# Gated linear attention's projections as seven block products in four passes over the tokens

## The chip, the cores and the metric

The kernel runs on one core of a Trainium2 chip. The metric is the device time of one execution in microseconds (us). The core has five engines, each with its own instruction queue: TensorE (PE; matmuls, with a sequencer that loads the held operand), VectorE (DVE), ScalarE (ACT), GpSimd (POOL) and SyncE (SP, which here issues almost all transfers). They meet through semaphores. Data lies in HBM and is moved to on-chip SBUF by 16 DMA engines; matmuls write to PSUM, 8 banks of 128 x 512 floats.

## What is computed

One layer, float32, on x of 2048 tokens by 1024. Attention first, then an FFN:

```python
h = rmsnorm(x, mix_norm_w)
q, k, v, r, glr = split(h @ w_in, [512, 1024, 2048, 3072])     # 4 heads, dk 128, dv 256, gate rank 16
log_a = log_sigmoid(glr @ w_gate2 + b_gate) / 16
g = cumsum of log_a within chunks of 64 tokens;  k_dec = k * exp(g_end - g)
for each chunk c:  state = state * exp(g_end[c]) + k_dec[c].T @ v[c];  o[c] = (q[c] / sqrt(128)) @ state
x = x + (rms_normalize(o) * norm_w * silu(r)) @ w_out
h = rmsnorm(x, ffn_norm_w);  u = causal_conv3(h @ w_up);  x = x + (silu(u[:2816]) * u[2816:]) @ w_down
out = rmsnorm(x, final_norm_w)
```

## The kernel before

Every float32 operand of a product is split into a high half in float32r and a low half, the rest (`split`, L206: a copy on ACT at L209, a subtraction on DVE at L210). A product then takes three matmuls per 128 of depth, high by low, low by high, high by high (`mm3`, L333; `mm3p`, L728).

Attention works on four blocks of 512 tokens. Per block x is normed and transposed (L354, L294), and its two halves stay in SBUF. Then for each head come r (`comp_r_tile`, tokens held, 256 columns moved; head 3 takes the gate's 16 columns along, 272), q (`comp_q`, weights held, 512 tokens moved) and k and v together (`comp_kv`, 384 columns). The weights are loaded and split anew for each block by `Weights` (L215), paced by a clock that `adv` moves on with each matmul (L315). The decay path (`phase_b2`, L384) turns gate values into factors and chunk sums. `scan_k` updates a head's state for the two chunks of a 128-token tile with two matmuls each, high and low half of k stacked in one operand; `scan_o` follows a delay of 4.5 us later (`later_do` with DLY), `scan_x` transposes the result for the output projection `comp_y` (L582), which runs in two halves of 512 columns. After the second half a tile is normed for the FFN, and `blocks` (L601) makes the seven operands of the FFN's products for a pair of tiles and stores them (`hd`, 14 stores of 256 KB).

The FFN already works in seven block products instead of eight: `phase_u` for up, conv and gate (two halves of 1024 tokens), then the down stage from `units` (L901) on. The tile scheduler adds the waits; each engine takes its instructions in the order in which the program emits them.

## Time and profile before

| | |
|---|---|
| median of 3 runs | 2247.65 us (2246.14 to 2248.06) |
| profiled execution, its own time | 2248.04 us |
| its span | 2246.3 us |
| granted TensorE clock, mean | 0.99 |
| attention, from the start to the first up product | 0 to 937.7 us |
| up stage | 937.7 to about 1816 us |
| down stage and final norm | about 1816 us to the end |
| DMA | 322.84 MB, mean 144 GB/s |

A group's row names a line, an engine, an operation, out<-in and a count, then busy us and the mean ns of one; behind the bar stands how long the engine had been idle before it, and who ended that. PE is TensorE's matmuls, PEld its weight loads. Matmuls overlap, so their mean is a latency; what one costs in a stream is the distance of two starts. L209 and L210 are the helper's lines, so their rows are told apart by the tiles.

### The profile page before, as it was taken

The page shows a single profiled execution, that of the slowest core. Times are in us where ns is not written, and L with a number is a line of the kernel's source. Part 1 is how long each engine was busy: PE and PEld are TensorE (multiplying, and loading weights), DVE is VectorE, ACT ScalarE, POOL GpSimd, SP SyncE. Part 2 cuts the span into 40 slices and gives each one's busy share as a digit, 9 for nine tenths or more (in the row PEclk, how much of TensorE's full clock was granted, in tenths as well). Part 3 has the DMA queues.
Part 4 walks back from the last instruction along what each step waited for, and adds up shares of the span by engine and source line. Part 5 has one row for each costly group of instructions (what it writes and reads, how often), then busy time and mean ns, then how long its engine had stood idle before and what let it go on. Part 6 is the DMA issues. An engine that isn't in the chain of part 4 may idle for free.

```text
span 2246.3 us, 31132 instructions
## 1 busy us (share of the span) xinstructions
PE 2172.5 (97%) x10909; PEld 1852.2 (82%) x10909; DVE 1519.6 (68%) x2337; ACT 1161.0 (52%) x2283; POOL 702.9 (31%) x639
## 2 busy tenths in 40 slices
...
GB/s 174 76 94 86 194 173 95 72 180 219 76 86 142 243 57 152 221 256 112 89 122 89 113 84 278 192 90 122 90 117 85 134 190 322 146 179 155 131 211 103
DMA packets 327886, 322.84 MB, mean 144 GB/s; under 512 B 15687, under 2 KB 262655, under 8 KB 324145
## 3 DMA queue, kind: packets, MB, share of 16 engines
...
q14 instruction: 73, 0.59, 0.1%
...
## 4 chain that ended last, share of the span: by engine, by line
PE 80%; DVE 7%; ACT 6%; issue 3%; DMA 3%; POOL 2%; SPq 0%; DVEq 0%; POOLq 0%; ACTq 0%
PE ua L733 7%; PE ua L734 7%; PE ua L735 7%; PE pd_p L735 6%; PE pd_p L734 6%; PE pd_p L733 6%; PE uc L733 4%; PE uc L734 3%; PE uc L735 3%; PE pkv L336 2%; PE pkv L338 2%; PE pkv L337 2%; PE pr L337 2%; PE pr L338 2%; PE pr L336 2%
## 5 line engine op out<-in xcount | busy, mean ns | idle before, releaser
L733 PE MATMUL ua<-h_p,uw_p 128*128 128x512 f32 x704 | 276.8, 393 | 1.2 <-DMA h_p<-hd_p 1.2
L735 PE MATMUL ua<-h_p,uw_p 128*128 128x512 f32 x704 | 276.3, 393 | 0.0
L734 PE MATMUL ua<-h_p,uw_p 128*128 128x512 f32 x704 | 276.2, 392 | 0.0
L806 DVE SCALAR_TENSOR_TENSOR t<-u,cw,t 128x1024 f32<-128x1024 f32 x176 | 244.2, 1418 | 40.4 <-ACT t L804 23.3
L735 PE MATMUL pd_p<-dw_p,da_p 128*128 128x512 f32 x616 | 239.6, 389 | 0.0
L734 PE MATMUL pd_p<-dw_p,da_p 128*128 128x512 f32 x616 | 239.6, 389 | 0.0
L733 PE MATMUL pd_p<-dw_p,da_p 128*128 128x512 f32 x616 | 239.6, 389 | 0.0
L210 DVE TENSOR_TENSOR uw_p<-us_p,uw_p 128x512 fp32r<-128x512 f32 x176 | 158.1, 900 | 118.4 <-ACT uw_p L209 118.4
L210 DVE TENSOR_TENSOR da_p<-da_p,da_p 128x512 fp32r<-128x512 f32 x154 | 127.7, 844 | 136.9 <-ACT da_p L209 134.8
L286 POOL TENSOR_TENSOR rstd_o<-var_o,neghalf 128x1 f32<-128x1 f32 x64 | 49.8, 778 | 535.2 <-DVE var_o L284 535.2
L209 ACT CAST uw_p<-us_p 128x512 fp32r<-128x512 f32 x176 | 108.5, 618 | 193.4 <-PE ua L734 75.5
L209 ACT CAST da_p<-da_p 128x512 fp32r<-128x512 f32 x154 | 94.1, 622 | 220.1 <-PE pd_p L734 171.1
L336 PE MATMUL pkv<-wl_q,hTh 128*128 128x384 f32 x512 | 172.6, 337 | 0.0
L338 PE MATMUL pkv<-wh_q,hTh 128*128 128x384 f32 x512 | 171.9, 336 | 0.0
L337 PE MATMUL pkv<-wh_q,hTl 128*128 128x384 f32 x512 | 171.5, 335 | 0.0
L733 PEld LDWEIGHTS ua<-h_p,uw_p 128*128 128x128 f32 x704 | 132.3, 188 | 31.8 <-issue 1.6
L735 PEld LDWEIGHTS ua<-h_p,uw_p 128*128 128x128 f32 x704 | 132.3, 188 | 30.1
L734 PEld LDWEIGHTS ua<-h_p,uw_p 128*128 128x128 f32 x704 | 132.3, 188 | 30.0
L733 PE MATMUL uc<-h_p,uw_p 128*128 128x512 f32 x352 | 142.4, 404 | 8.9 <-DVE u L886 7.7
L336 PE MATMUL pr<-wl_r,hTh 128*128 128x256 f32 (+1 forms) x512 | 150.1, 293 | 0.1
L337 PE MATMUL pr<-wh_r,hTl 128*128 128x256 f32 (+1 forms) x512 | 146.3, 286 | 0.4 <-DVE hTl L210 0.3
L210 DVE TENSOR_TENSOR uw_p<-ur,uw_p 128x512 fp32r<-128x512 f32 x132 | 129.3, 992 | 24.7 <-ACT uw_p L209 24.7
(208 smaller groups left out, 5661.2 us busy)
## 6 DMA issues: line engine op xcount, KB each, us to landing
...
da_p<-ad_p SPq DMA_DIRECT2D x154, 256.0 KB, 3.3
hd_p<-h_p SPq DMA_DIRECT2D x112, 256.0 KB, 3.6
...
ad_p<-as_p SPq DMA_DIRECT2D x88, 256.0 KB, 3.2
dr_p<-in_ffn_w_down_dram SPq DMA_DIRECT2D x77, 256.0 KB, 3.2
ad_p<-t SPq DMA_DIRECT2D x66, 256.0 KB, 4.6
raw_q<-in_gla_w_in_dram SPq DMA_DIRECT2D x128, 128.0 KB, 2.3
```

The costliest lines, as they stand in the source:

```text
L209: nc.scalar.copy(hi, src)
L210: nc.vector.tensor_sub(lo, src, f32(hi))
L286: nc.gpsimd.tensor_tensor(rstd, var, neghalf, op=ALU.pow)
L336: nc.tensor.matmul(ps_ap, ah, bl, start=(i == 0), stop=False)
L337: nc.tensor.matmul(ps_ap, al, bh, start=False, stop=False)
L338: nc.tensor.matmul(ps_ap, ah, bh, start=False, stop=(i == n - 1))
L733: nc.tensor.matmul(ps_ap, ah, bl, start=(first and i == 0), stop=False, **kw)
L734: nc.tensor.matmul(ps_ap, al, bh, start=False, stop=False, **kw)
L735: nc.tensor.matmul(ps_ap, ah, bh, start=False, stop=(last and i == len(pairs) - 1), **kw)
L806: nc.vector.scalar_tensor_tensor(t, u[:, k:k + TS], cw[:, k, c:c + 1], t, op0=ALU.mult, op1=ALU.add)
```

## The change

Attention runs as four passes over all 2048 tokens: R (r and the gate), A (k, q, v of heads 0 and 1), B (heads 2 and 3), Y (output). A pass has 1024 columns and a depth of 1024, both cut in two; with a pair of token tiles that is a 2 x 2 x 2 block product, taken as seven products (p1 to p7) of sums and differences of blocks, 12 matmuls each. `prep_w` makes a pass's seven weight operands (sums on POOL, splits on ACT and DVE), which stay in SBUF for the pass's eight units; in the last unit of a pass each is replaced by the next pass's, as its product is done. `prep_row` makes the token side: in R from the normed x, stored to HBM as well (`h1d`), in A and B by loading these, in Y from the attention rows. r, the decay factors and the attention rows go through HBM (`rd`, `ed`, `od`). The gate gets matmuls of its own (`gate_mm`), the chunk sums as well (`sums`). The scan takes two heads of a tile at once: three matmuls per head and chunk for the state, and q is transposed from rows (`scan_tile`). The norm weight is multiplied into silu(r) on POOL instead of into the output weights. The FFN keeps its order; its operand ring has 6 pairs (18 single buffers before), its activations lie in the buffers that held the passes' weights and are loaded in the last Y unit.

```diff
-    HEADS = [3, 0, 1, 2]
-    WB = 18
-    SB = 13
...
+    NTT = S // P
+    NP = NTT // 2
+    WB = 6
+    RB = 4
+    SB = 8
+    YB = 7
+    LEAD = 4
+    DLY = 4.5
+    TX0, TX = (16.4, 18.6), (10.8, 13.5)
...
-    class Weights:
...
-    def comp_r_tile(b, h, hT, tt, rs):
-        pr = mm_ps(f"pr_{b}_{h}_{tt}")
...
-    def comp_q(b, h, hT):
-        pq = mm_ps(f"pq_{b}_{h}")
-        mm3(pq, KT, ((w_q(b, h, kt, 0, DK), hs(hT, kt, slice(0, T))) for kt in range(KT)))
...
-    def scan_k(b, h, tt, n, kk, vv, vl, dec, rs, oT):
-        S_ = []
-        for c in range(2):
-            pk = aux_ps(f"pk_{n}_{c}")
-            nc.tensor.matmul(pk[:, :DV], kk[:, c, :], vl[:, c, :], start=True, stop=False)
-            nc.tensor.matmul(pk[:, :DV], kk[:, c, :], vv[:, c, :], start=False, stop=True)
...
+    def w_block(ps_, i, j):
+        ks = slice(HK * j, HK * (j + 1))
+        if ps_ == "R":
+            return [(0, wv[:, ks, OR + 512 * i:OR + 512 * (i + 1)])]
+        if ps_ == "Y":
+            return [(0, wov[:, ks, 512 * i:512 * (i + 1)])]
+        g = "AB".index(ps_)
+        if i == 1:
+            return [(0, wv[:, ks, OV + 512 * g:OV + 512 * (g + 1)])]
+        return [(0, wv[:, ks, OK_ + 256 * g:OK_ + 256 * (g + 1)]), (256, wv[:, ks, OQ + 256 * g:OQ + 256 * (g + 1)])]
...
+    WSRC = {"p1": ((0, 0),), "p5": ((1, 0), (1, 1)), "p6": ((0, 0),), "p2": ((0, 1),), "p3": (), "p7": ((0, 0), (1, 0)), "p4": ((1, 1),)}
+    WHALF = [(o, k, ij) for o in PORD for k in range(2) for ij in WSRC[o]]
...
+    def load_w(ps_, n):
+        while wload.get(ps_, 0) < min(n, len(WHALF)):
+            m = wload.get(ps_, 0)
+            o, k, ij = WHALF[m]
+            r = wgot[ps_, o, k, ij] = raw_tile([P, 2, 512], f"wr_{ps_}_{m}")
+            for c, src in w_block(ps_, *ij):
+                nc.sync.dma_start(r[:, :, c:c + src.shape[-1]], src[:, 2 * k:2 * k + 2, :])
+            wload[ps_] = m + 1
...
+    def stage_w(ps_, o, ijs):
+        t = uh.tile([P, KT, 512], F32, tag=o, name=f"ws_{ps_}_{o}", bufs=1)
+        for n, ij in enumerate(ijs):
+            for c, src in w_block(ps_, *ij):
+                nc.sync.dma_start(t[:, n * HK:(n + 1) * HK, c:c + src.shape[-1]], src)
+            staged[ij] = t[:, n * HK:(n + 1) * HK, :]
...
+    def prep_w(ps_, o):
+        t = uh.tile([P, KT, 512], F32R, tag=o, name=f"w_{ps_}_{o}", bufs=1)
+        hi, lo = t[:, :HK, :], t[:, HK:, :]
+        for k in range(2):
+            v = (slice(None), slice(2 * k, 2 * k + 2))
+            r = [wgot.pop((ps_, o, k, ij)) if (ps_, o, k, ij) in wgot else staged[ij][v] for ij in WSRC[o]]
+            src = xsum[v]
+            if o == "p5":
+                nc.gpsimd.tensor_add(src, *r)
+            elif o == "p6":
+                nc.gpsimd.tensor_sub(src, src, r[0])
+            elif o == "p7":
+                nc.gpsimd.tensor_sub(r[1], *r)
+                src = r[1]
+            elif o != "p3":
+                src = r[0]
+            split(hi[v], lo[v], src)
+            if o == "p2":
+                nc.gpsimd.tensor_sub(xsum[v], r[0], xsum[v])
+        W[ps_, o] = (hi, lo)
...
+    def split_row(ps_, j, o, src):
+        t = w_pair(f"h_{ps_}{j}_{o}")
+        split(t[:, 0, :], t[:, 1, :], src)
+        if ps_ == "R":
+            nc.sync.dma_start(h1d[j, o], f32(t))
+        rows[ps_, j, o] = t[:, 0, :], t[:, 1, :]
...
+    def norm_x(t):
+        xt = xin[t]
+        junk = gp.tile([P, 1024], BF16, tag="cp", name=f"junk_{t}", bufs=4)
+        rstd = rstd_of(xt, D, f"a{t}", junk, "a")
+        nc.vector.scalar_tensor_tensor(xt, xt, rstd, rp["nw"], op0=ALU.mult, op1=ALU.mult)
...
+        b11, b21 = hsrc.pop(("t", t - 1))
+        b12, b22 = hsrc.pop(("t", t))
+        t1 = diff(j, "p5", b12, b11)
+        t2 = diff(j, "p6", b22, t1)
+        diff(j, "p7", b22, b12)
+        hsrc[j, "p3"] = b22
+        hsrc["p4", j] = (b21, t2)
...
+    def prep_row(ps_, j, o):
+        if ps_ == "R":
+            need(f"h{j}")
+            if o == "p4":
+                diff(j, o, *hsrc.pop(("p4", j)))
+            split_row(ps_, j, o, hsrc.pop((j, o)))
+        elif ps_ in "AB":
+            t = w_pair(f"h_{ps_}{j}_{o}")
+            nc.sync.dma_start(f32(t), h1d[j, o])
+            rows[ps_, j, o] = t[:, 0, :], t[:, 1, :]
...
+                t = oraw[j, o] = cp_tile(f"ot_{j}_{o}")
+                a, c = {"p5": (b12, b11), "p6": (b22, oraw.get((j, "p5"))), "p7": (b22, b12), "p4": (b21, oraw.get((j, "p6")))}[o]
+                nc.gpsimd.tensor_sub(t, a, c)
+            else:
+                t = {"p1": b11, "p2": b21, "p3": b22}[o]
+            split_row(ps_, j, o, t)
...
+    def gate_mm(j, o, hh, hl):
+        if o not in ("p1", "p5", "p2", "p3"):
+            return
+        GR = 2 * RANK
...
+        k0 = HK if o in ("p2", "p3") else 0
+        for c in {"p1": (0, 1), "p5": (1,), "p2": (0,), "p3": (1,)}[o]:
+            out = pg[:GR, c * P:(c + 1) * P]
+            kw = {} if o == "p1" and c == 0 else {"skip_group_check": True}
+            for k in range(HK):
+                ks = slice(k * P, (k + 1) * P)
+                nc.tensor.matmul(out, wg[:, 1, k0 + k, :], hl[:, ks], start=(o == "p1" and c == 0 and k == 0), stop=False, **kw)
+                nc.tensor.matmul(out, wg[:, 0, k0 + k, :], hh[:, ks], start=False, stop=(k == HK - 1), **kw)
...
+            for h in range(H):
+                for i in range(2):
+                    nc.tensor.matmul(pe[:, 2 * h:2 * h + 2], L[tt][1 - i][:, h * DK:(h + 1) * DK], rp["chunk"], start=(i == 0), stop=(i == 1))
...
+    def scan_loads(g, t):
+        e = sp["a"].tile([P, 2 * DK], F32, tag="E", name=f"E_{g}_{t}", bufs=2)
...
+        r = sp["a"].tile([P, 512], F32, tag="r", name=f"r_{g}_{t}", bufs=2)
+        nc.sync.dma_start(r, rd[t][g])
+        nc.scalar.activation(r, r, AF.Silu)
+        nc.gpsimd.tensor_mul(r, r, sp["gnw"])
+        er[t] = e, r
...
+        def first():
+            e, box["r"] = er.pop(t)
+            kd = sp["a"].tile([P, 2 * DK], F32, tag="kd", name=f"kd_{n}", bufs=1)
+            nc.vector.tensor_mul(kd, kq[:, :2 * DK], e)
+            for c in range(2):
+                own = slice(c * CH, (c + 1) * CH)
+                split(kz[0][own, c, :], kz[1][own, c, :], kd[own, :])
+            pq = aux_ps(f"pq_{n}")
+            for h in range(2):
+                nc.tensor.transpose(pq[:, h * P:(h + 1) * P], kq[:, (2 + h) * DK:(3 + h) * DK], ident)
...
+        def scan_k():
+            state = sp["state"]
+            for c in range(2):
+                pk = aux_ps(f"pk_{n}_{c}")
+                for h in range(2):
+                    kh, kl = (kz[i][:, c, h * DK:(h + 1) * DK] for i in range(2))
+                    vh, vl = (v[i][:, h * DV:(h + 1) * DV] for i in range(2))
+                    o = pk[:, h * DV:(h + 1) * DV]
+                    nc.tensor.matmul(o, kh, vl, start=True, stop=False)
+                    nc.tensor.matmul(o, kl, vh, start=False, stop=False)
+                    nc.tensor.matmul(o, kh, vh, start=False, stop=True)
+                    adv(0.36)
...
+                for h in range(2):
+                    nc.vector.scalar_tensor_tensor(state[:, h, :], state[:, h, :], dec[:, 2 * g + h, ci:ci + 1], pk[:, h * DV:(h + 1) * DV], op0=ALU.mult, op1=ALU.add)
+                sh = sp["b"].tile([P, 2, DV], F32R, tag=f"sh{c}", name=f"sh_{n}_{c}", bufs=1)
+                sl = sp["b"].tile([P, 2, DV], F32R, tag=f"sl{c}", name=f"sl_{n}_{c}", bufs=1)
+                split(sh, sl, state)
+                S_.append((sh, sl))
+            later_do(DLY, scan_o)
...
+        def scan_o():
+            po = aux_ps(f"po_{n}")
+            for h in range(2):
+                pairs = [((q[0][:, h, c * CH:c * CH + P], q[1][:, h, c * CH:c * CH + P]), (S_[c][0][:, h, :], S_[c][1][:, h, :])) for c in range(2)]
+                mm3p(po[:, h * DV:(h + 1) * DV], pairs)
...
+    def unit(ps_, j):
...
+        first = ps_ == "R" and j == 0
+        if ps_ == "R":
+            if first:
+                wload[ps_] = len(WHALF) - 2
+                load_w(ps_, len(WHALF))
+            elif j + 2 < NP:
+                for t in (e + 4, d + 4):
+                    xin[t] = load_x(t, "x")
+            if j + 1 < NP:
+                for i, t in enumerate((e + 2, d + 2)):
+                    norm_x(t)
+                    later_do((TX0 if first else TX)[i], lambda t=t: blocks_x(t))
...
+        if ps_ == "Y":
+            xe, xd = xin.pop(e), xin.pop(d)
...
+        if j + 1 == NP and nxt:
+            load_w(nxt, RB)
+        for i, o in enumerate(PORD):
+            if first:
+                for m in range(WEARLY[i], WEARLY[i + 1]):
+                    prep_w(ps_, PORD[m])
+                    prep_rows(m + 1)
+            prep_rows(limit(ps_, j, i))
...
+            hh, hl = rows.pop((ps_, j, o))
+            wh, wl = W[ps_, o]
+            pairs = [((hh[:, k * P:(k + 1) * P], hl[:, k * P:(k + 1) * P]), (wh[:, k, :], wl[:, k, :])) for k in range(HK)]
+            if o in ("p1", "p5", "p2"):
+                a = bank[o] = mm_ps(f"m{o}_{ps_}_{j}")
...
+            else:
+                a = bank["p5" if o == "p3" else "p1"]
+                mm3p(a, pairs, first=False, more=True)
+            if ps_ == "R":
+                gate_mm(j, o, hh, hl)
+            if j + 1 == NP:
+                if nxt:
+                    load_w(nxt, WEND[i - 1] + RB if i else 0)
+                    prep_w(nxt, o)
...
+                else:
+                    load_op(0, o)
+                    if i == 3:
...
+            if ps_ == "Y":
+                for xt, cs in {"p1": ((xe, c1),), "p5": ((xd, c2),), "p6": ((xd, c1),), "p2": ((xe, c1),),
+                               "p7": ((xd, c2),), "p3": ((xd, c1),), "p4": ((xe, c2),)}[o]:
+                    add(xt[:, cs], xt[:, cs], a)
+                if o == "p7":
+                    x1_done(d, xd)
+                if o == "p4":
+                    x1_done(e, xe)
+                continue
...
+            if o in ("p1", "p5", "p6"):
+                keep[o] = cp_tile(f"c{o}_{ps_}_{j}")
+                nc.scalar.copy(keep[o], a)
+            elif o == "p2":
...
+                elif o == "p4":
+                    ve = scan_v(g, e, a)
+                    scan_loads(g, d)
+                    if j > 0 or g > 0:
+                        need(*(f"scan{g if j else 0}_{(e - 1 - k) % NTT}" for k in range(2)))
+                    if j == 0:
+                        scan_b(g)
+                    later_do(0.2, lambda: scan_tile(g, e, o11, ve, lambda: scan_tile(g, d, o12, keep["vd"], lambda: None)))
...
+    rp["h"] = rp["hctx"].enter_context(tc.tile_pool(name="rh", bufs=1, side="right"))
+    rp["nw"] = rp["h"].tile([P, D], F32, name="nw_mix")
+    nc.sync.dma_start(rp["nw"], mix_norm_w.partition_broadcast(P))
+    xin[1] = load_x(1, "x")
...
+    stage_w("R", "p4", ((0, 0), (1, 0)))
+    stage_w("R", "p7", ((1, 1), (0, 1)))
+    gate_weights()
+    xin[2], xin[3] = load_x(2, "x"), load_x(3, "x")
+    for t in range(2):
+        norm_x(t)
...
+    nc.gpsimd.memset(halo, 0.0)
+    later_do(12.0, vectors)
+    for ps_ in PS:
```

917 lines of the change are left out of this document (413 added, 504 removed).

## The prediction

> **What bounds the kernel now.** The page was read first (its busy table and its chain of waits), then the busy time by stretches of the span, then the groups by line, then single instructions in order of time.
>
> ```profile
> span 2246.3 us, 31132 instructions
> ...
> PE 2172.5 (97%) x10909; PEld 1852.2 (82%) x10909; DVE 1519.6 (68%) x2337; ACT 1161.0 (52%) x2283; POOL 702.9 (31%) x639
> ...
> PE 80%; DVE 7%; ACT 6%; issue 3%; DMA 3%; POOL 2%; SPq 0%; DVEq 0%; POOLq 0%; ACTq 0%
> ```
>
> TensorE is the bound: 97% busy and 80% of the chain. Attention ends where the first FFN product starts, at 937.7 us (the tile ua's row: ns, then first and last start):
>
> ```profile
> L733 PE MATMUL ua<-h_p,uw_p x704: 387/392/632, 937.7 to 1812.7; 128*128 128x512 f32 x176
> ```
>
> The stretches (columns: time, then busy us and instructions of PE, weight loads, DVE, ACT and POOL, granted clock, DMA share, GB/s):
>
> ```profile
> 0.00:20.00 20.00, 9.30 (x54) 8.78 (x55) 10.70 (x21) 11.12 (x23) 8.96 (x34) 1.00 0.88 267
> 20.00:40.00 20.00, 19.65 (x123) 17.11 (x122) 11.95 (x32) 15.36 (x34) 0.93 (x1) 1.00 0.70 208
> ...
> 260.00:270.00 10.00, 7.07 (x25) 4.12 (x23) 9.23 (x12) 8.18 (x17) 3.09 (x3) 0.77 0.94 267
> 270.00:280.00 10.00, 9.08 (x40) 7.24 (x41) 5.56 (x11) 5.08 (x11) 2.62 (x2) 0.71 0.98 292
> 280.00:290.00 10.00, 8.85 (x51) 8.45 (x50) 8.17 (x15) 6.12 (x15) 3.75 (x3) 1.00 1.12 333
> ...
> 0.00:938.00 938.00, 891.13 (x5351) 807.75 (x5352) 613.86 (x1334) 578.68 (x1381) 123.13 (x156) 0.99 0.44 137
> ...
> 937.00:1040.00 103.00, 87.54 (x360) 69.92 (x359) 80.41 (x78) 47.20 (x76) 55.02 (x47) 0.92 0.65 205
> 1040.00:1800.00 760.00, 756.67 (x3276) 613.25 (x3275) 569.40 (x586) 374.36 (x551) 407.98 (x348) 1.00 0.39 124
> ```
>
> A busy figure counts overlapping latencies, so what a matmul costs is read from start to start. The FFN's up stage, which already works in seven block products, gives 760/3276 = 0.232 us per 512-wide matmul. Attention's own, from matmuls in a row (start, duration, line, operands), and their numbers from the groups:
>
> ```profile
> 52.71 0.41 PE L434 MATMUL pdec<-ident,dc 8*128 8x8 f32 x4 [0.22 <-ACT dc L428]
> ...
> 130.01 0.33 PE L336 MATMUL pkv<-wl_q,hTh 128*128 128x384 f32 x1
> ...
> 131.91 0.33 PE L338 MATMUL pkv<-wh_q,hTh 128*128 128x384 f32 x1
> ...
> 899.56 0.28 PE L337 MATMUL po<-sh,qlo 128*128 128x256 f32 x1
> ...
> 900.15 0.40 PE L336 MATMUL py<-wl_o,oTh 128*128 128x512 f32 x1
> ...
> 904.79 0.40 PE L338 MATMUL py<-wh_o,oTh 128*128 128x512 f32 x1
> 905.03 0.38 PE L577 MATMUL px<-ident,og 128*128 128x128 f32 x2
> 905.17 0.48 PE L336 MATMUL py<-wl_o,oTh 128*128 128x512 f32 x1
> ```
>
> ```profile
> L336 PE MATMUL pkv<-wl_q,hTh 128*128 128x384 f32 x512 | 172.6, 337 | 0.0
> ...
> L336 PE MATMUL pr<-wl_r,hTh 128*128 128x256 f32 (+1 forms) x512 | 150.1, 293 | 0.1
> ...
> L336 PE MATMUL py<-wl_o,oTh 128*128 128x512 f32 x256 | 103.1, 405 | 0.2
> ...
> L337 PE MATMUL pq<-hTh,wl_q 128*128 128x512 f32 x128 | 53.7, 419 | 10.3 <-DVE wl_q L210 10.3
> ...
> L336 PE MATMUL po<-sl,qhi 128*128 128x256 f32 x128 | 38.8, 303 | 9.6 <-DVE sl L210 7.6 <-DVE var_a L284 1.5 <-DVE var_o L284 0.4
> ...
> L554 PE MATMUL pk<-vlz,kk 128*128 128x256 f32 x128 | 35.0, 293 | 5.0 <-DVE vlz L547 3.8 <-DVE state L558 0.9
> ...
> L577 PE MATMUL px<-ident,og 128*128 128x128 f32 x128 | 25.3, 276 | 1.2 <-DVE og L571 1.2
> ...
> L607 PE MATMUL pt_d<-ident,h 128*128 128x128 f32 x128 | 18.8, 289 | 13.5 <-DVE h L598 10.6 <-DVE var_d L284 3.0
> ...
> L423 PE MATMUL pge<-ll,inchunk 128*8 128x512 f32 x16 | 7.0, 435 | 0.0
> ...
> L434 PE MATMUL pdec<-ident,dc 8*128 8x8 f32 x16 | 1.6, 207 | 0.2 <-ACT dc L428 0.2
> ```
>
> So: 384 wide, 11 steps in 1.90 us, 0.173; 256 wide, 5 steps in 0.59, 0.118; 512 wide, 20 steps in 4.64, 0.232; two transposes 0.14; the smallest, (0.41 - 0.207)/3 = 0.068. At these prices attention holds 836 us of TensorE work: 1536 k-v matmuls 265, 1536 gate-branch ones (taken as 256 wide) 181, 768 output ones 178, 384 q ones 89, 384 + 256 of the scan 76, 128 scan transposes 9 and 256 token transposes 18, 80 of the decay path 19, 16 small 1. It takes 938, so **102 us are lost** to waits and to a lowered clock: the start, and above all the block ends, where the output projection, the FFN's operands and their stores meet (260 to 280 us: clock 0.77 and 0.71, DMA share 0.94 and 0.98).
>
> **The change part by part.** *Projections.* Seven products of 12 matmuls for two token tiles by 1024 columns, 32 such units: 2688 matmuls of 512 columns at 0.232 = 624 us, against 265 + 181 + 178 + 89 = 713. **-89.**
>
> *Scan of two heads.* Its output matmuls stay 384; the state products go from 256 to 384, since the high and low halves of k are no longer stacked in one operand: 128 x 0.118 = +15. q now leaves the product with tokens on the partitions and is transposed: 64, in pairs of 0.14, +4.5.
>
> *Gate.* The gate's 16 columns leave the product and become 320 matmuls, 128 wide with 32 columns held. No row shows this form. Below it stands the smallest matmul, 0.068 (22 us), above it the 256-wide one, 0.118 (38), or at the very worst the 512-wide one, 0.232 (74). I take 0.068, as the 256-wide one is twice the columns. The chunk sums become 128 matmuls of two columns (0.068, +9) for 32 of 512 (-7) and 16 transposes (-1). Together +23. TensorE's work thus falls by 89 - 15 - 4.5 - 23 = **-46 us**, to 790.
>
> By the Trainium skill, "TensorE: Matmul & The Clock Gate", section Back-to-back issue gap, pairs of weight load and matmul sustain about 81 ns at 128 columns; the small transposes here show 68 ns; by the page's figure the gate would be 4 us dearer, an estimate, and the sum the same within its range.
>
> What is lost to waits comes anew, from these prices (the second fence is from the transfers: KB of one, us to landing):
>
> ```profile
> L210 DVE TENSOR_TENSOR uw_p<-ur,uw_p 128x512 fp32r<-128x512 f32 x132 | 129.3, 992 | 24.7 <-ACT uw_p L209 24.7
> ...
> L209 ACT CAST uw_p<-us_p 128x512 fp32r<-128x512 f32 x176 | 108.5, 618 | 193.4 <-PE ua L734 75.5 <-PE ub L734 40.0 <-POOL us_p L762 37.3
> ...
> L210 DVE TENSOR_TENSOR wl_q<-raw_q,wh_q 128x512 fp32r<-128x512 f32 x128 | 89.1, 710 | 7.5 <-ACT wh_q L209 5.5 <-PE pr L338 0.2
> ...
> L762 POOL TENSOR_TENSOR us_p<-ur 128x512 f32<-128x512 f32 x44 | 75.6, 1719 | 25.8 <-DMA ur<-in_ffn_w_up_dram 16.7 <-DVE uw_p L210 8.7
> ...
> L558 DVE SCALAR_TENSOR_TENSOR state<-state,dec,pk 128x256 f32<-128x256 f32 x128 | 60.7, 474 | 2.8
> ...
> L762 POOL TENSOR_TENSOR us_p<-ur,ur 128x512 f32<-128x512 f32 x44 | 60.3, 1374 | 19.5 <-DVE uw_p L210 19.5
> ...
> L210 DVE TENSOR_TENSOR h_p<-ht_p,h_p 128x512 fp32r<-128x512 f32 x32 | 33.8, 1055 | 3.3 <-ACT h_p L209 1.6 <-DMA hd_p<-h_p 0.6
> ...
> L598 DVE SCALAR_TENSOR_TENSOR h<-x,rstd_d,nw_ffn 128x1024 f32<-128x1024 f32 x16 | 26.7, 1666 | 10.1 <-POOL rstd_d L286 10.1
> ...
> L593 DVE TENSOR_TENSOR x<-x,py 128x512 f32<-128x512 f32 x32 | 21.9, 683 | 20.6 <-PE py L338 20.3
> ```
>
> ```profile
> hd_p<-h_p SPq DMA_DIRECT2D x112, 256.0 KB, 3.6
> ```
>
> *The start.* ACT and POOL get the norms of tiles 2 and 3 ahead of the first weights (`norm_x` stands before the loop in `unit`), and SP issues those two loads behind 4.2 MB of weights: 7.0 MB in all, at 267 GB/s from 2 us on, 28 us. Only then come the splits and POOL's chain of weight sums (p5, p6, the sum behind p2, p7): 8 halves of 2 x 1.37 to 2 x 1.72, some 3.1 us each, 25 us. First product near 31, p7 near 57, the unit's end near 61, for 26 us of TensorE work: **35 lost.** It is bounded below by 20 (the loads alone), above by 50 (POOL at 1.72, and the products, which wait in turn, at a lowered clock). The old start lost its share too; it is in the 102.
>
> *Pass changes (R to A, A to B, B to Y).* In the last unit of a pass the next pass's weights are made: 16 loads of 512 KB through four buffers, 14 splits of 1024 columns, POOL's 25 us. SP's loads wait for a buffer that POOL frees; queued behind them are the operand rows of the next unit, which TensorE needs. DVE has 14 x 1.3 = 18 us more there, on top of a unit's own work in a window of 26. Spread over two units it nearly fits; the rest falls on scans that wait for DVE. From 0 (all hidden) to 18 each; I take 20 for the three.
>
> *The Y pass.* A unit is 84 x 0.232 + 16 transposes, 20.6 us of TensorE. DVE has 7 row splits at 0.95 (between 0.71 and 0.99, nearer the row with POOL at work), 7 adds at 0.68, two norms at 1.67, 7 operand splits at 1.06: 22 us. DMA has 6.8 MB (7 x 512 KB of FFN operands, 1 MB each of attention rows, x and its sum's store; one store of 256 KB lands in 3.6 us): at 290 GB/s 23.5. Both above TensorE, so a unit takes 25: 8 x 4.4 = **35 lost**; from 0 to 64 (28.7 us, 6.8 MB at 238 GB/s, the mean of the first two stretches).
>
> *The scan's wait.* A scan tile now updates two heads: per chunk two state updates of 0.474, a split of 0.618 and 0.71, twice 2.28 = 4.6 us in a row on DVE and ACT, where one head took half; the delay before the output matmuls is still 4.5 us of TensorE work, and behind a waiting output matmul stands the next unit's product. Before, the output matmuls waited 9.6 us for 64 heads' tiles (row of po). For 32 double tiles I bound it by 0 and 32 (1 us each) and take 0.3 each, 10; with 2 for other gaps in R, A and B, **12 lost**.
>
> Lost: 35 + 20 + 35 + 12 = 102, as before by chance; the block ends go, and a dearer start and pass changes come. The early FFN (937 to 1040: 360 matmuls, 84 us' worth, in 103) I leave alone: its operands now load in the last Y unit, whose 15 MB crowd the same queue. The FFN's shorter ring, six pairs for nine, has five jobs of lead, 14 us, as its cover; without it DVE's stalls would show, 750 us of matmuls at 1% being 8. **Sum: -46**, from the profiled execution's 2248.0 us (2246.3 is its span; the median of the runs is 2247.65): **2202 us.**
>
> **The rivals.** *A, the losses fall.* If Y is bound by TensorE and the pass changes hide, 35 + 12 + 5 are lost instead of 102: 2152. For it: DVE is at 65% and POOL at 13% over 0 to 938 us, so there is room on average. Against it: the Y pass, where three engines stand at their limits in one window.
>
> *B, slower: transfers bind attention.* Operand rows are stored and read twice, gates, r and attention rows go out and back, weights come four times. By the shapes that is 50 MB in R, 40 each in A and B, 55 in Y and 30 of weights: 215 MB, against 938 x 137 = 128 MB now, all on SP's queue. It decides where the queue carries less than 215 MB / 942 us = 228 GB/s. At 220 attention takes 977 us: 2287. For it: 208 GB/s at 20 to 40 us. Against it: 333 at 280 to 290, and 267 to 292 where stores of the same kind press.
>
> *C, no change: the weights' preparation paces the pass changes.* POOL and DVE then sit at their upper prices at the start and at all three changes: 50 + 54 + 35 + 12 = 151 lost, 2251. For it: POOL's 1.72 and DVE's 0.99 are what the up stage pays when both work. Against it: the next pass's first products need only the first weights, so most of the chain has a second unit to finish in.
>
> That the change does not shorten TensorE's list of projections at all can be left out: the numbers of matmuls are fixed by the loops.
>
> **How the numbers follow.** Forecast 0.57, A 0.21, B 0.16, C 0.06 (the likeliest decides the time). About 0.2%, 4.5 us, is what a measurement of this kernel tells from no change. Faster: forecast and A, 0.78; same: C, 0.06; slower: B, 0.16. The likeliest case by itself spans 2165 to 2240, with the bounds of start, changes and Y partly offsetting. The range reaches past A below, and above past C and a gate at its worst (52 more, 2254) towards B: 2145 to 2262.
>
> **What would show it.** Right: attention's end near 890 us; 2688 projection matmuls near 0.23 us start to start; the first one near 31 us, with ACT waiting for the x loads; POOL as the releaser of p5 to p7 in the first 60 us; in the Y pass DVE over 85% busy and a DMA share over 0.9. Wrong: gate matmuls over 0.12 us; a DMA share near 1 in the A and B passes with TensorE waiting for operand rows (B); a Y unit near 21 us (A); an up stage longer than 880 us.

## The result, and the profile after

The change makes the kernel slower: 2361.43 us (2359.31 to 2364.44) against 2247.86 us, a ratio of 1.0508 with an interval of 1.049 to 1.0526. The forecast was 2202 us, faster. The page of the kernel after (span; busy time; shares of the chain of waits):

```profile
span 2357.6 us, 28614 instructions
...
PE 2142.0 (91%) x9948; PEld 1764.0 (75%) x9948; DVE 1571.2 (67%) x1967; ACT 1052.0 (45%) x1837; POOL 926.2 (39%) x730
...
PE 47%; DVE 6%; DMA 3%; issue 3%; POOL 2%; ACT 2%; SPq 0%; DVEq 0%; POOLq 0%; ACTq 0%
```

TensorE has less to do (2142 us busy for 2172, 961 matmuls fewer), yet it is 91% busy instead of 97%. The shares of the chain can't be set against the 80% of before: here they add up to 63%, since the chain could be followed back only as far as about 865 us, into the Y pass. The stretches by stage, from the starts of the first products (columns as in the prediction: time, then busy us and instructions of PE, weight loads, DVE, ACT and POOL, granted clock, DMA share, GB/s). The rows are the start (first unit of R), the rest of R, A, B, Y, the first 92 us of the up stage, its rest, and the down stage:

```profile
0.00:73.60 73.60, 36.53 (x160) 28.10 (x161) 59.79 (x55) 28.91 (x40) 42.68 (x36) 0.79 0.51 181
73.60:300.40 226.80, 198.48 (x1089) 162.29 (x1089) 124.84 (x156) 118.38 (x207) 63.14 (x45) 0.92 0.62 222
300.40:533.70 233.30, 215.99 (x1121) 183.31 (x1120) 129.76 (x250) 114.05 (x245) 50.74 (x44) 0.96 0.64 210
533.70:782.30 248.60, 225.76 (x1180) 190.65 (x1179) 151.89 (x295) 112.94 (x261) 61.71 (x45) 0.96 0.61 203
782.30:1004.00 221.70, 185.67 (x832) 150.03 (x831) 159.84 (x209) 98.25 (x178) 101.75 (x77) 0.93 0.73 236
1004.00:1096.00 92.00, 61.12 (x257) 48.93 (x256) 50.38 (x55) 35.71 (x58) 34.70 (x33) 0.83 0.71 236
1096.00:1927.40 831.40, 796.58 (x3458) 651.75 (x3457) 635.79 (x624) 398.17 (x587) 448.11 (x365) 0.99 0.39 124
1927.40:2357.60 430.20, 421.90 (x1861) 348.96 (x1860) 258.88 (x328) 145.62 (x263) 123.35 (x89) 0.99 0.51 175
```

And the up and down stages before:

```profile
937.70:1030.00 92.30, 81.19 (x344) 64.85 (x342) 70.66 (x70) 43.74 (x72) 48.72 (x42) 0.94 0.68 217
1030.00:1816.20 786.20, 778.52 (x3357) 630.86 (x3358) 590.60 (x611) 386.20 (x568) 413.57 (x354) 1.00 0.39 125
1816.20:2246.30 430.10, 422.00 (x1861) 348.95 (x1859) 244.83 (x325) 152.42 (x264) 117.72 (x89) 0.99 0.51 178
```

Attention ends at 1004.0 instead of 937.7 us: +66. The up stage takes 923.4 us instead of 878.5: +45. The down stage is the same. That is the whole 111 us by which the spans differ. What TensorE waits for (releaser: us in total, times, longest):

```profile
PE mp_Y L170 <- DVE x L786: 30.5, 7, 5.8
PE px L609 <- DVE og L602: 30.4, 19, 6.6
PE uc L170 <- DVE u L969: 30.2, 20, 2.8
PE ua L170 <- ACT uw_p L177: 19.1, 1, 19.1
PE pz L448 <- ACT gstk L432: 14.7, 4, 7.3
...
PE pg L424 <- DVE wg L392: 10.8, 1, 10.8
```

There is no single large wait but some in each stage: Y, the scan, the up stage in its course and at its head, the gate in R, the start. And a wait can cost more than its length. Two instances, in R and in Y (start, duration, line, operands; in brackets the idle time and its releaser), where the product p4 waits for the reading of p7 (in Y the scheduler has put half a dozen matmuls of the next unit between the two):

```profile
131.05 0.39 PE L170 MATMUL mp_R<-w_R_p,h_R_p 128*128 128x512 f32 x1
133.82 0.80 PE L170 MATMUL mp_R<-w_R_p,h_R_p 128*128 128x512 f32 x1 [2.38 <-DVE o_R L741]
134.42 0.63 PE L171 MATMUL mp_R<-w_R_p,h_R_p 128*128 128x512 f32 x1
...
136.55 0.63 PE L170 MATMUL mp_R<-w_R_p,h_R_p 128*128 128x512 f32 x1
...
883.95 0.39 PE L170 MATMUL mp_Y<-w_Y_p,h_Y_p 128*128 128x512 f32 x1
...
889.16 0.39 PE L172 MATMUL mp_Y<-w_Y_p,h_Y_p 128*128 128x512 f32 x1
894.74 0.74 PE L170 MATMUL mp_Y<-w_Y_p,h_Y_p 128*128 128x512 f32 x1 [5.19 <-DVE x L786]
```

Before the wait in Y, 23 steps take 5.21 us, 0.227 each. After the wait in R, five steps take 2.13 us from 134.42 on, 0.43 each: the granted clock is 0.50 from 133.66 to 137.07 us, so the pause of 2.4 costs 1.5 us more.

At the prediction's way of pricing (start to start: 0.228 for 512 columns, 0.119 for 256, 0.06 to 0.11 for the small ones) attention holds about 782 us of matmuls, against the forecast's 790. It takes 1004, so **222 us are lost where 102 were forecast**: start 48, rest of R 50, A 30, B 38, Y 56 (length of the stage less its matmuls' price).

### The profile page after: what moved, and what is told of

It is laid out like the page before. It is cut to its first block, busy times and chain, and to the rows that moved or that the text cites. A ratio compares the mean times of both kernels' runs of the same rounds, so it can differ in the third digit from the quotient of the medians.

```text
span 2357.6 us, 28614 instructions
## 1 busy us (share of the span) xinstructions
PE 2142.0 (91%) x9948; PEld 1764.0 (75%) x9948; DVE 1571.2 (67%) x1967; ACT 1052.0 (45%) x1837; POOL 926.2 (39%) x730
## 2 busy tenths in 40 slices
DMA packets 320640, 415.39 MB, mean 176 GB/s; under 512 B 19166, under 2 KB 212878, under 8 KB 316912
## 3 DMA queue, kind: packets, MB, share of 16 engines
q8 instruction: 78, 1.28, 0.2%
## 4 chain that ended last, share of the span: by engine, by line
PE 47%; DVE 6%; DMA 3%; issue 3%; POOL 2%; ACT 2%; SPq 0%; DVEq 0%; POOLq 0%; ACTq 0%
PE pd_p L171 6%; PE pd_p L170 6%; PE pd_p L172 6%; PE ua L172 5%; PE ua L171 5%; PE ua L170 5%; PE uc L170 3%; DVE t L896 3%; PE uc L171 3%; PE uc L172 3%; PE ub L172 2%; PE ub L170 2%; PE ub L171 2%; DVE uw_p L178 1%; DMA ur<-in_ffn_w_up_dram 1%
## 5 line engine op out<-in xcount | busy, mean ns | idle before, releaser
L170 PE MATMUL ua<-h_p,uw_p 128*128 128x512 f32 x704 | 276.8, 393 | 35.5 <-ACT uw_p L177 19.1
L896 DVE SCALAR_TENSOR_TENSOR t<-u,cw,t 128x1024 f32<-128x1024 f32 x176 | 261.3, 1513 | 21.7 <-POOL halo L892 9.4
L170 PE MATMUL pd_p<-dw_p,da 128*128 128x512 f32 x616 | 239.6, 389 | 0.0
L171 PE MATMUL pd_p<-dw_p,da 128*128 128x512 f32 x616 | 239.6, 389 | 0.0
L172 PE MATMUL pd_p<-dw_p,da 128*128 128x512 f32 x616 | 239.6, 389 | 0.0
L178 DVE TENSOR_TENSOR uw_p<-ur,uw_p 128x512 fp32r<-128x512 f32 x132 | 140.7, 1066 | 94.4 <-ACT uw_p L177 92.9
L178 DVE TENSOR_TENSOR da<-da_p,da 128x512 fp32r<-128x512 f32 x154 | 127.0, 879 | 105.7 <-ACT da L177 105.6
L177 ACT CAST da<-da_p 128x512 fp32r<-128x512 f32 x154 | 85.2, 618 | 204.1 <-PE pd_p L172 162.8
L170 PE MATMUL uc<-h_p,uw_p 128*128 128x512 f32 x352 | 141.4, 402 | 30.2 <-DVE u L969 30.2
L878 ACT COPY c<-ua 128x512 f32<-128x512 f32 x132 | 77.0, 584 | 146.8 <-PE ua L172 145.2
L171 PE MATMUL uc<-h_p,uw_p 128*128 128x512 f32 x352 | 139.1, 395 | 0.0
L172 PE MATMUL uc<-h_p,uw_p 128*128 128x512 f32 x352 | 139.0, 395 | 0.0
L170 PEld LDWEIGHTS pd_p<-dw_p,da 128*128 128x128 f32 x616 | 115.7, 188 | 24.2
L172 PEld LDWEIGHTS pd_p<-dw_p,da 128*128 128x128 f32 x616 | 115.7, 188 | 23.9
L171 PEld LDWEIGHTS pd_p<-dw_p,da 128*128 128x128 f32 x616 | 115.7, 188 | 23.9
```

The costliest lines, as they stand in the source:

```text
L170: nc.tensor.matmul(ps_ap, ah, bl, start=(first and i == 0), stop=False, **kw)
L171: nc.tensor.matmul(ps_ap, al, bh, start=False, stop=False, **kw)
L172: nc.tensor.matmul(ps_ap, ah, bh, start=False, stop=(last and i == len(pairs) - 1), **kw)
L177: nc.scalar.copy(hi, src)
L178: nc.vector.tensor_sub(lo, src, f32(hi))
L878: nc.scalar.copy(t, pa)
```

## The experiments

Times are of one execution each unless an interval is given; gains are against the kernel after, 2361.43 us, where nothing else is said. The kernel before, timed beside them, took 2247.8 to 2251.6 us, and the end of R lies anywhere from 295 to 302 us in runs that change nothing before it; differences below 6 us are not read.

**Y: is it DVE's work, or POOL's place in the order?** In Y the row differences go from POOL to DVE:

```diff
-                nc.gpsimd.tensor_sub(t, a, c)
+                nc.vector.tensor_sub(t, a, c)
```

> The four differences per Y unit that make the token operands (`prep_row`, L357) move from POOL to DVE; all else stays, the result too. Theory P: the Y pass (226 us, 20.6 us of TensorE work per unit of 28) waits because POOL makes eight differences per unit in one run of 13 us, ACT and DVE stand in order behind the one that is not ready, and DVE's additions that free the PSUM banks come late. Then the stall of 5 to 6 us at the head of each unit shrinks to under 2 and the Y pass falls to about 195 us; the time falls by 25 to 35 us against the changed kernel. Theory D (the forecast): DVE's own 22 us per unit are the bound; 4 more operations of 0.7 to 1.0 us per unit make Y longer, 235 to 255 us. Theory T: transfers bind Y; then nothing moves by more than 5 us.

2333.91 us, 27 less, as theory P gave. Y itself takes 198.8 us for 221.7; the rest lies ahead of the edited code. DVE does more (164.57 us busy for 159.84) and is done sooner, so its load was not the limit. POOL's run in front of the wait shown above, and DVE's queue beside it, in the kernel after:

```profile
881.16 1.74 POOL L357 TENSOR_TENSOR ot_p<-ob,ob 128x512 f32<-128x512 f32 x1
...
889.20 1.71 POOL L664 TENSOR_TENSOR h2t_p<-hb,hb 128x512 f32<-128x512 f32 x1
...
883.59 1.55 DVE L178 TENSOR_TENSOR h_Y_p<-ot_p,h_Y_p 128x512 fp32r<-128x512 f32 x1
...
891.60 0.69 DVE L178 TENSOR_TENSOR h_p<-h2t_p,h_p 128x512 fp32r<-128x512 f32 x1 [1.21 <-ACT h_p L177]
...
894.01 0.68 DVE L786 TENSOR_TENSOR x<-x,mp_Y 128x512 f32<-128x512 f32 x1
```

POOL works through eight differences in a row, 878.2 to 890.9. ACT's splits of h2t stand behind the last of them, DVE's splits behind ACT's, and the addition that reads p7's sum stands behind those on DVE; it runs at 894.01, and p4 starts at 894.74. DVE's subtraction of 128x512 takes 1.55 us while POOL works, 0.69 after POOL has finished.

**The stores in Y.** Only the high halves of the FFN's operands are stored, and loaded twice:

```diff
-            for i in range(2):
+            for i in range(1):
                 nc.sync.dma_start(hd[s, o, i][:, :, j // 2 * P:(j // 2 + 1) * P], f32(hl[i])...
```

> Left out: the low halves of the FFN's operands are not stored in the Y pass (7 stores of 256 KB fewer per unit), and the up stage loads the high half twice instead, so the FFN computes with wrong low halves; the instructions on the engines and the bytes of the loads stay. Theory T (stores of 512-byte pieces bind the Y pass): a unit's transfers fall from 6.8 to 5.0 MB, Y falls from 226 to near 200 us. Theory P (POOL's run of differences and the order behind it): Y stays within 8 us of 226. In both the early up stage may gain up to 10 us, since fewer stores stand in the queue there.

2345.55 us, 16 less. Y takes 212.2 us for 221.7, between what the two theories gave, and the up stage 913.2 for 923.4, since its two first waits fall from 19.1 and 11.1 us to 8.5 and 8.0. Transfers have a share in both places, and are the whole of neither.

**What the pass changes cost.** A, B and Y use R's weights; their loads, sums and splits are left out, and the output with them:

```diff
-                    load_w(nxt, WEND[i - 1] + RB if i else 0)
-                    prep_w(nxt, o)
+                    W[nxt, o] = W[ps_, o]
```

> Left out: the weights of passes A, B and Y are neither loaded nor split; R's seven operands serve all four passes, so attention's values are wrong. It measures the three pass changes as a whole. Forecast's step: they cost 20 us. From the trace of the changed kernel (the last and first units of R to B take 37, 42, 34, 46 us against 27 in between): 45 to 65 us less. If the rest of the loss came from elsewhere (the scan), under 15.

2305.71 us, 56 less. The stretches of A and B in this run:

```profile
287.20:507.60 220.40, 214.00 (x1129) 182.24 (x1128) 108.38 (x244) 100.16 (x235) 28.03 (x34) 0.98 0.57 182
507.60:730.00 222.40, 215.44 (x1171) 183.92 (x1171) 119.40 (x271) 94.64 (x237) 33.55 (x35) 1.00 0.55 175
```

R is 13 us shorter, A 13, B 26: the three changes cost about **52 us** (R's part by itself is uncertain by some 5), where the forecast took 20 of at most 54.

**The up stage's ring.** Nine pairs again, every third from the up stage's own pool:

```diff
-            t = w_pair(f"uw_{s}_{f}_{o}")
+            if "us" in pools and k % 3 == 2:
+                t = pools["us"].tile([P, 2, 512], F32R, tag="w2", name=f"uw_{s}_{f}_{o}", bufs=3)
+            else:
+                t = w_pair(f"uw_{s}_{f}_{o}")
```

> The up stage gets nine pairs of weight operands again, as before the change (three more in a pool of their own, every third job); attention is untouched. Theory U1: the ring of six is what costs the up stage about 2 us in each group of 14 products (PE waits for DVE there), because a split can start only when the product six jobs back is done; then the 1.9 us gaps go, and the up stage from 1090 us on (837 us) falls by 25 to 35 us. Theory U2: the gaps come from DVE being slower there (1513 against 1418 ns in the convolution) or from other buffers; then under 8 us.

2340.41 us, 21 less, of which the up stage has 14 (909.4 us for 923.4) and the rest lies ahead of the edited code: more than theory U2 gave, and less than U1. What SP's queue waits for in the up stage (1100 to 1800 us), first in the kernel after, then with nine pairs:

```profile
SPq L907 <- DVE t L903: 374.3, 17, 26.6
SPq L846 <- DVE uw_p L178: 83.6, 46, 25.7
```

```profile
SPq L846 <- DVE uw_p L178: 362.6, 66, 15.9
```

With the short ring SP stands up to 26.6 us at a store of activations (L907), and the loads of the next weights behind it; with nine pairs most of its waiting is at the loads (L846), as in the kernel before. The lead that was to cover the shorter ring went into this wait on SP.

**The weights' sums on DVE.**

```diff
-                nc.gpsimd.tensor_add(src, *r)
+                nc.vector.tensor_add(src, *r)
```

and the three other sums of `prep_w` likewise.

> The eight sums and differences of each pass's weights (prep_w, 1024 columns each) go from POOL to DVE; nothing is left out. Theory Q, POOL's queue: at the pass changes the scan's small power (rstd, L599) stands on POOL behind weight sums of 2.4 to 2.9 us, the scan's transposes px wait for it (29.6 us in A and B, 10.3 where no weights are made), and at the start the chain of sums ends at 49.5 us. Then the changes lose 15 to 30 us less and the start 5 to 12: 2320 to 2341 us. Theory W, DVE's own work and the loads pace a change: the sums add 8 x 1.35 = 11 us of DVE to each of four windows, and the time stays within 6 us or rises by up to 20: 2355 to 2381 us.

2323.09 us, 38 less: start 7, rest of R 6, A 16, B 8. That is theory Q. DVE gets eight operations more at each change and is still ahead, as POOL's sums (2.4 to 3.1 us each) no longer hold the scan's small power behind them: TensorE's waits for px in the change from A to B fall from 10.6 us to 3.1.

**The head of the up stage, by order.** The first up weights are asked for ahead of the FFN's operands:

```diff
-                    load_op(0, o)
-                    if i == 3:
+                    if i == 0:
                         ux["u"] = phase_u(0)
                         next(ux["u"])
+                    load_op(0, o)
```

> The four loads of the first up weights are issued at the start of the last Y unit, ahead of the 14 MB of FFN operands, instead of between the fourth and the fifth of them. Theory E1, order in SP's queue: the 20 us gap at 1010 us (the first up product waits on ACT's split, that on the load) goes, 12 to 20 us: 2341 to 2350 us. Theory E2, volume: 14 MB have to come in anyway, the gap moves to the operands of the later products, and the time stays within 6 us: 2355 to 2367 us.

2373.77 us, no gain (12 more, about half of it ahead of the edit). The waits from 1009 to 1110 us:

```profile
PE ua L170 <- DVE u L962: 21.9, 1, 21.9
PE ua L170 <- DMA h_p<-hd_p: 7.5, 2, 5.2
```

The 19 us of waiting for the weights are gone; waits for DVE's u and for operands have come in their place. So order alone is not it; the time is 7 us past the range of theory E2. In the kernel after the DMA share is 1.04 to 1.07 from 1010 to 1030 us, while TensorE waits for the weights, which speaks for volume there; in the second wait, 1060 to 1070 us, it is 0.49. Of the runs only the one with fewer stores cut TensorE's waits in the first 100 us of the up stage clearly, from 30.8 us to 17.4.

**The gate in R.** Its first matmuls later (`TB0` 1.0 to 6.0).

> In pass R the first gate matmuls of a block (pz) are put 6.0 us of TensorE work behind the operand they read, instead of 1.0 (TB0); the rest of the decay path moves along. Theory C1, cover too short: the pz waits (14.7 us in four) and the lowered clock behind each go: 10 to 22 us less, 2339 to 2351 us. Theory C2: the chain of ACT and DVE behind pz is what is late, the wait turns up at pd (5 us now) or at pass A, which needs all the decay factors: within 5 us, 2356 to 2366 us.

2367.45 us, no gain: theory C2, just past its edge. R's waits at 74 to 345 us:

```profile
PE mp_R L170 <- DVE o_R L741: 19.1, 5, 8.2
PE mp_R L170 <- ACT cp_R L794: 15.1, 4, 4.9
```

The pz waits are gone, and mp_R's, 10.7 us there in the kernel after, are 34.2: the wait has moved to the reading of R's own sums by ACT's copies and DVE's additions.

**All wide sums on DVE** (R's rows and the FFN's operands too, `gpsimd` to `vector` in `diff` and `blocks`).

> All wide sums and differences of attention and of the FFN operands' making (weights, rows in R and in Y, FFN operands) go from POOL to DVE; nothing is left out. Theory Q: POOL's length and place in the order is what costs, DVE has room (65% busy over attention): this adds the gains of moving Y's rows (27) and the weights' sums, with 10 to 20 more for R's rows and the FFN operands: 2285 to 2320 us. Theory D: with 8 more operations of 0.68 us per unit DVE becomes the bound of R and Y (in Y 22 + 8 x 0.68 = 27.5 us per unit, where units take 25 with half of it moved): no better than moving Y's rows alone, 2330 us or more.

2278.55 us, 83 less, 6 us more than theory Q gave at most: start 11, rest of R 21, A 8, B 9, Y 38, and 7 lost again in the up stage. R's split of a row, from 74 to 300 us in the kernel after, with POOL's difference that runs beside it; and in this run from 62 to 267 us, with DVE's own difference:

```profile
L178 DVE TENSOR_TENSOR h_R_p<-ht_p,h_R_p 128x512 fp32r<-128x512 f32 x26 | 26.3, 1013 | 24.1 <-ACT h_R_p L177 23.2
...
L300 POOL TENSOR_TENSOR ht_p<-hb,ht_p 128x512 f32<-128x512 f32 x13 | 19.8, 1520 | 0.5
```

```profile
L178 DVE TENSOR_TENSOR h_R_p<-ht_p,h_R_p 128x512 fp32r<-128x512 f32 x26 | 17.9, 689 | 16.1 <-ACT h_R_p L177 15.9
...
L300 DVE TENSOR_TENSOR ht_p<-hb,ht_p 128x512 f32<-128x512 f32 x13 | 8.9, 683 | 0.0
```

A difference of 512 columns takes 1520 ns on POOL and 683 on DVE, and DVE's split falls from 1013 to 689 ns on average when POOL is quiet; what stands behind a difference waits 0.8 us less. In the whole of the kernel after, the 16 of these splits that overlap a wide POOL operation take 1166 to 1768 ns and the other 16 take 680 to 694: DVE's split is slow only while POOL works beside it. The Trainium skill, "SBUF — State Buffer", section Who interferes with whom, says that a DVE instruction with two SBUF inputs and a GpSimd instruction that reads SBUF share a port, and that the second to start waits for the first; these rows agree.

**Both together** (all sums on DVE, nine pairs).

> All wide sums of attention on DVE (as before in the run that took 2278.6 us) and the up stage's operand ring at nine pairs again. If the causes are separate, their gains add: the ring alone took 14 us from the up stage, so 2260 to 2268 us. If the ring's gain came from the same stalls of DVE, 2272 us or more.

2265.53 us: the ring's gain adds. On top of it, **a longer cover for the scan's transposes**, `later_do(DLY, scan_x)` to 8.5 us, og and ot sharing two buffers:

> As the run with all sums on DVE and nine pairs, and the scan's transposes (scan_x) follow the output matmuls after 8.5 us of TensorE work instead of 4.5 (og and ot share two buffers). Theory S, the scan's cover: at the pass changes the scan's last step stands on DVE behind weight splits of 1.2 us and sums of 1.2 us, and TensorE waits at px (6.7 us at once in the change from B to Y); twice the cover takes most of this, 6 to 15 us. Theory W, DVE's own work paces the change (27 us of splits and sums in a unit of 27 us): the wait moves on to the next product, within 4 us of the run without it.

2261.18 us, 4 less, on the border of the two theories and below what is read. In the change from B to Y px still waits 6.7 us at once: DVE is 31.40 us busy in 33 there (694 to 727 us of the run with all sums on DVE), so there was little room for the wait to go. And on top of the pair, **SP's order at the head of the up stage**: the weights first, and the last pair's operand stores on ACT's queue:

```diff
-                nc.sync.dma_start(hd[s, o, i][...
+                (nc.scalar if tt == NTT - 2 else nc.sync).dma_start(hd[s, o, i][...
```

> As the run with all sums on DVE and nine pairs; the first four loads of up weights are issued ahead of the FFN operands' loads, and the FFN operand stores of the last pair of tiles (14 of 256 KB) go through ACT's queue instead of SP's. Theory E3, SP's order held the early up stage twice, first the weights behind 14 MB of operands, then (second stall, 10 to 22 us, waiting for DVE's u) the last pair's stores behind the same 14 MB, whose buffers the up stage has to wait for: both go, 12 to 22 us less than without. Theory E2, volume: some 20 MB at 350 to 400 GB/s take 50 us whatever the order, within 5 us.

2266.92 us, no gain. This is within theory E2's range: TensorE now waits 21.0 us there for the operands' transfers, where it waited for the weights. No order of the same transfers was found that shortens that window.

**The order of two products.** In `unit` p7 and p4 add into the same PSUM bank one after the other, and p4 must wait until p7's sum has been read:

```diff
-    PORD = ("p1", "p5", "p6", "p2", "p3", "p7", "p4")
+    PORD = ("p1", "p5", "p6", "p2", "p7", "p3", "p4")
...
-                if o == "p7":
+                if o == "p3":
                     x1_done(d, xd)
```

> Only the order of two products is changed: p3 comes between p7 and p4 (PORD p1, p5, p6, p2, p7, p3, p4), and a tile's last sum in Y moves with it. Theory B, one bank: p7 and p4 add into the same PSUM bank back to back, so p4 waits until p7's sum has been read by DVE, however late DVE is (2.4 us at 131 us in R, 5.2 us at 889 us in Y), and the granted clock is low for some eight matmuls after; in A and B the scan's matmuls lie between. With 2.7 us of p3 as cover R loses 15 to 30 us less and Y 15 to 40: 2296 to 2331 us. Theory L, lateness: DVE and ACT are late by themselves and the wait only moves to the next product: within 8 us, 2353 to 2369 us.

2345.36 us, 16 less than after, between the ranges of the two theories, and not where it was expected: A and B have 9 of it (a steady unit takes 26.2 us for 27.0), Y 3, R none: there, counted from one, the even units are 4 to 5 us shorter and the odd ones from the third on 2 to 5 us longer. R's waits from 60 to 300 us, Y's largest wait, and ACT's queue in one odd unit of R:

```profile
PE mp_R L170 <- ACT cp_R L794: 20.2, 5, 5.0
...
PE mp_Y L170 <- ACT h_p L177: 18.9, 4, 5.5
```

```profile
225.29 1.09 ACT L450 ACTIVATE e<-pz 128x512 f32<-128x512 f32 x2
...
227.44 1.28 ACT L455 ACT_TABLE_LOAD   x1
...
236.17 0.60 ACT L177 CAST lh<-e 128x512 fp32r<-128x512 f32 x1
236.68 0.58 ACT L794 COPY cp_R<-mp_R 128x512 f32<-128x512 f32 x1
```

In R the wait has moved to p6, which needs the bank that ACT's copy (L794) has to read; the copy stands behind the decay path's softplus, which ACT works through in one stretch from 225.3 to 236.2 us. In Y the waits for the reading of p7 (30.5 us) are gone, and 24.5 us of waits that end with ACT's splits have come: there the bank was only where the lateness of POOL, ACT and DVE showed, which is theory L. Put on top of the sums on DVE, the nine pairs and the cover, the order gives:

> All wide sums on DVE, nine pairs in the up stage, the longer cover ahead of the scan's transposes (2261.2 us so far) and p3 between p7 and p4. Theory B: R still loses 28 us and Y 17; 8 to 20 us of it go: 2241 to 2253 us. Theory L: within 4 us, 2257 to 2265 us.

2246.55 us, 15 less: 10 in A and 6 in B, and not in R (5 more) or Y (1 less), where theory B had put them. And with half of the weights' sums on POOL again:

> As the run before it, but of each pass's eight weight sums the four of the first half are on POOL again. If DVE's own work (27 us of splits and sums in a unit of 27 us) paces start and changes, 5 us less of it each time gives 4 to 12 us less than the run with all on DVE; if a wide POOL operation in the scan's way is what costs, whatever DVE has to do, 4 to 15 us more.

2270.83 us, 24 more: 6 at the start, 13 in A. Taking this work off DVE makes start and changes dearer, although DVE has less to do: the second theory's way, and 9 us beyond its range.

**R's copies on DVE**, alone with the new order, and with everything:

```diff
-                nc.scalar.copy(keep[o], a)
+                (nc.vector.tensor_copy if ps_ == "R" else nc.scalar.copy)(keep[o], a)
```

> As the run with only p3 put between p7 and p4 (2345.4 us), and pass R's copies of a product's sum out of PSUM (cp_R, L794) go from ACT to DVE. Theory G, ACT's order: in every second unit of R the copy stands on ACT behind the decay path's softplus (11 us in one run at 225 us, with three table loads of 1.28 us), p6 adds into the same bank and waits 5.0 us with a lowered clock behind; the odd units fall from 38 us towards 31, pass R loses 16 to 28 us less: 2317 to 2330 us. Theory L, lateness of ACT and DVE as such: the wait goes to the operand splits, within 6 us, 2339 to 2351 us.

> The run with all sums on DVE, nine pairs, the longer cover and p3 between p7 and p4 (2246.6 us), and pass R's copies on DVE as well. Theory G: the odd units of R (37.4 us) fall by 4 to 7 us, four of them: 2218 to 2231 us, 0.9 to 1.5% below the kernel before. Theory L, DVE has all the sums already and the copies come late there too: within 6 us, 2240 to 2252 us, the same as the kernel before.

2339.78 us, 6 less than without, and 2248.77 us, a ratio of 0.9995 (0.9986 to 1.0004) to the kernel before: the same. Both lie in the range of theory L. The odd units of R still take 35 to 38 us. DVE's queue in the second of these runs:

```profile
212.22 1.29 DVE L456 SCALAR_TENSOR_TENSOR e<-pz,e 128x512 f32<-128x512 f32 x2 [3.79 <-ACT e L455]
213.42 0.68 DVE L794 COPY cp_R<-mp_R 128x512 f32<-128x512 f32 x1
```

The copy has changed queues and stands behind the same chain, since the softplus has a DVE step that waits for ACT.

**The softplus in parts**, on top of all that. Its second half follows after 8.0 us instead of 2.0, and its DVE step is issued 5.5 us behind its ACT steps; the splits and the chunk sums behind it are spread accordingly (the sums 3.5 us apart instead of 2.5):

```diff
-            for i, e in enumerate(es[-2:]):
+            for e in es[-2:]:
                 nc.scalar.activation(e, e, AF.Ln, bias=1.0)
-                nc.vector.scalar_tensor_tensor(e, pzs[i], 0.0, e, op0=ALU.min, op1=ALU.subtract)
+            later_do(5.5, lambda: rest(half, pzs))
...
-        later_do(t0 + 2.0, lambda: softplus(1))
+        later_do(t0 + 8.0, lambda: softplus(1))
```

> The run with all edits and pass R's copies on DVE (2248.8 us, the same as the kernel before), and the decay path's softplus of a block is cut: its second pair of tiles comes 8.0 us behind the first instead of 2.0, its DVE step 5.5 us behind its ACT steps, the sums from 10 us on every 3.5 us. Theory G, one run of 11 us on ACT holds ACT and, through the DVE step that waits for it, DVE: R's four odd units fall from 37 us to 30 to 33: 2230 to 2240 us. Theory L: R's odd units hold 6 us more of TensorE work and more of ACT and DVE, and wait elsewhere: within 5 us, 2244 to 2254 us.

> The run before it (2233.8 us), in which one DVE step of the last block of tokens came behind the reading of its result; here each block's splits wait in the program's order for that step (need), the amount of work is the same. Theory G: the gain came from cutting the run of 11 us on ACT: 2230 to 2238 us, a ratio of 0.991 to 0.996 to the kernel before. The rival: it came from the last block's wrong order, which let pass A begin earlier: 2243 to 2251 us, the same as before.

In the first of the two runs the last block's splits read values whose DVE step comes too late, so its result is wrong: 2233.82 us, the median of five. In the second the splits wait for that step: 2230.83 us (2229.95 to 2234.49), a ratio of **0.9918 (0.9904 to 0.9932)**, as theory G gave. The odd units of R take 31.2 us for 35 to 38. This version is 0.8% shorter than the kernel before. Its start, R, A, B, Y, and the two stretches of its up stage:

```profile
0.00:60.70 60.70, 35.14 (x161) 26.63 (x162) 49.41 (x67) 27.56 (x37) 7.33 (x20) 0.94 0.69 237
60.70:259.20 198.50, 187.93 (x1099) 156.66 (x1098) 143.29 (x216) 110.06 (x190) 6.99 (x12) 0.98 0.69 251
259.20:472.30 213.10, 209.09 (x1111) 177.87 (x1109) 126.66 (x252) 108.73 (x237) 29.37 (x36) 0.98 0.70 226
472.30:707.50 235.20, 219.69 (x1183) 185.68 (x1180) 165.25 (x309) 117.33 (x266) 38.50 (x36) 0.98 0.68 219
707.50:891.00 183.50, 177.76 (x842) 144.99 (x843) 163.02 (x272) 96.71 (x180) 14.38 (x18) 0.99 0.89 282
891.00:983.00 92.00, 60.17 (x251) 48.05 (x250) 56.84 (x62) 36.25 (x60) 31.72 (x29) 0.83 0.76 251
983.00:1797.80 814.80, 800.03 (x3453) 647.66 (x3452) 595.42 (x620) 396.38 (x583) 429.89 (x364) 1.00 0.39 125
```

Attention ends at 891.0 us, where the prediction had it (890), but that bears the prediction out only in the sum, and is in part luck: this is another kernel, and at the same prices it loses about 35 us at the start, 57 in R, A and B where 32 were forecast, and 18 in Y where 35 were. The up stage, 906.8 us, still takes 28 more than before, and with them the time is 2230.8 and not 2202.

## Why the prediction was wrong

The forecast of TensorE's own work held; what it loses to waits was put at 102 us in attention, where it is 222, and at nothing in the up stage, where it is 45. The step that failed most is the term "12 lost" for the scan's wait and all other gaps in R, A and B: 66 were lost there beside the pass changes (118 less 52). Point by point, by its own steps:

- *TensorE's work falls by 46 us.* Right: 782 us by the trace, forecast 790. Projections 0.227 to 0.23 us each as taken; the gate's 320 matmuls come at 0.060 (15 steps from 140.02 to 140.92 us), below the lower bound of 0.068, and the chunk sums' at 0.11, above the 0.068 taken for them; the two errors offset each other. The change does what it says.
- *The start, 35 lost (20 to 50).* 48. The first product came at 14.3 us, not 31. The step rested on the program's order of norms and loads, and an engine's queue does not keep that order, contrary to what the section on the kernel before says: ACT squares a tile of the second pair at 52.3 us, behind splits that the program emits after it. POOL's chain of sums did hold p5 to p7, up to 49.5 us, as the step said: ACT's splits wait for it, 21 us in six waits. The wait for the gate's weights (10.8 us), which stand on DVE behind such splits, was not in it.
- *Pass changes, 20 lost.* Mis-sized: 52 by the run that keeps the weights, near the upper end of 54. "Spread over two units it nearly fits" counted each engine's work against a window. What failed is order: the scan's small steps stand behind sums and splits of 1.2 to 3.1 us on POOL and DVE, and TensorE behind them. With the sums off POOL, R, A and B are 30 us shorter; the rest of the 52 was not taken apart.
- *The Y pass, 35 lost (0 to 64), DVE over 85%, DMA share over 0.9.* 56, inside its bounds for another reason: DVE is busy 72% (159.84 of 221.7 us) and the DMA share is 0.73. The time went into waits of TensorE at the end of a chain from POOL over ACT to DVE, in the kernel after at p4, which waits until p7's sum is read. With everything off that chain Y takes 183.5 us and DMA reaches 0.89: only then is the forecast's mechanism in sight.
- *The scan's wait, 12 lost with all other gaps in R, A and B.* The failed step: 66 lost. In the steady units of A and B it nearly holds: they take 27.0 us for 25.8 of matmuls, 0.8 of the rest being p7 and p4. R was given its part of the 2 us for "other gaps" and lost 37 beside the change to A. Two things that other instructions stand behind were not priced. One is POOL's differences of the token rows: with all wide sums on DVE the rest of R is 21 us shorter, 15 more than with the weights' sums alone. The other is the decay path, as a run of 11 us on ACT: cut in parts, it makes R 12 us shorter. The prediction lists the decay path's matmuls alone.
- *The up stage left alone, the ring covered by 14 us of lead.* Wrong by 45, and 923 us is past the 880 that the prediction named as a sign of being wrong. The ring cost 14, at the place where SP waits. The head cost about 20, an estimate: in its first 92 us 257 matmuls run instead of 344. That "15 MB crowd the same queue" was seen and given no price. Some 10 us are left without a cause: with nine pairs the stage's rest still runs at 817 us for 3464 matmuls, 0.236, against 0.234 before.

The start cost 13 us more than forecast, the changes 32, Y 21, the scan and the gaps 54: together 120. With 782 for 790 and 45 for the up stage that makes 2202 + 120 - 8 + 45 = 2359 of the 2361 measured.

Of the rivals, B had the right sign and the wrong cause: 92.6 MB more are moved (415.39 against 322.84), about as it said, but at shares of 0.5 to 0.73 of the queue, and no wait for operand rows shows in A or B. C, weights at their upper prices, was nearest in mechanism (start and changes at 100 us, it had 104) and had the other losses too small.

What the experiments show and what they don't: that POOL's wide operations (83 us together), the six pairs of the ring (13 to 14), the order of p7 and p4 in A and B (9 alone, 16 on top of the rest) and the run of softplus (18) are causes is shown by taking each away. Together with the smaller edits they are 131 us; the forecast missed by 159. How POOL's cost is shared between the length of its operations, their place in the order and the slower DVE beside them was not separated. That DVE's splits are slower only beside POOL is shown; that the port is why is an inference from the durations. What holds the head of the up stage stays open: two runs with another order gained nothing, and fewer stores gained 10 us in the stage.
